# Output weights from three real products a direction, and the last quarter's Toeplitz blocks and early halves placed ahead of the late halves

## The chip, the cores and the metric

One core of one Trainium2 chip runs the kernel. The metric is the device time of one execution in microseconds (us); the kernel before took 1014.47 us, the median of three runs (1013.78 to 1017.83). The core has five instruction streams: PE (matmuls), DVE, ACT and POOL (element-wise work) and SP (which issues transfers only; ACT and POOL issue some as well). Each stream is executed in the order in which it was written, and streams wait for each other by semaphores.

## The reference

One layer: a bidirectional S5 mixer over 1024 tokens with a prefix of 256 context tokens, then a SwiGLU FFN and a final norm. The part that matters here is the S5 mixer, run once forward and once on the reversed sequence:

```python
lam_bar = jnp.exp(lam * jnp.exp(log_step)[:, None])
b_bar = ((lam_bar - 1.0) / lam)[..., None] * lax.complex(b_re, b_im)
bu = jnp.einsum('lgh,gnh->lgn', u, b_bar)
a = jnp.broadcast_to(lam_bar, bu.shape)
_, h = lax.associative_scan(_linear_combine, (a, bu), axis=0)   # h[l] = lam_bar h[l-1] + bu[l]
y = jnp.einsum('lgn,ghn->lgh', h, c_mat).real
...
g = jax.nn.gelu(y + d_skip * u)
return g * jax.nn.sigmoid(g @ w_glu + b_glu)
```

There are 64 groups of 16 channels with 64 complex states each. Everything is float32; the large matmuls run in fp32r with a high and a low part.

## The kernel before, in words

**Tokens and the scan.** The 1024 tokens stand as 128 columns of T = 8 tokens each. The recurrence runs over columns only (32 of context, 128 of tokens), both directions at once. After a loop of 16 blocks (`sums(hb)`, to about 123 us) has made each column's input, `scan()` runs on DVE alone: 95 steps of small TENSOR_TENSORs (L77 is the helper `tt`, which issues every TENSOR_TENSOR). A part of the columns is stepped through, the others are filled in from them on DVE and POOL.

**From states to outputs.** The groups come in eight parts k = 0..7 of 8, two parts to a quarter q = 0..3. A quarter needs three things. (1) Output weights `CL[q]`, one complex number for each direction, group, token of a column and channel: the complex output matrix C times powers of lam_bar. `cl_ops` makes them: a real or an imaginary part of one direction is the sum of two products of 128x1024, both made on POOL, one into its place and one into a scratch `ct`; with two directions that is eight products and four additions a quarter. (2) Lag matrices: `k_mats` (K) multiplies `CL[q]` by B-bar on PE (L809, L813, L817), ACT copies two results out (L821) and stores them to DRAM as `kd` (L822, issued by ACT); `toeplitz` (T, L830, issued by SP) reads them back as Toeplitz blocks into four slots `KQ`, two blocks for a k. (3) `x_mm` (L946) multiplies inputs by these blocks: the part of an output that comes from inside its own column. Then the states are multiplied by `CL[q]`: `states_mm` (L922) does one half of the columns, early or late; `states_all` (L935) does both. The backward direction needs a turned copy of the states (R early, Z late, z both; L902 on ACT, L904 on DVE).

**The additions of `cl_ops`** run on one of three engines, by a letter in the table `HOWS`: E on POOL itself; P on PE, as four identity matmuls into PSUM (L672) that ACT copies back (L673); Y by a DMA that POOL issues and that adds into its target (L675). Quarter 0 starts within the blocks of `sums`, with Y for its first two additions. In all POOL makes 9 additions, PE 5, the DMA 2.

**C's loads.** `cs_load(q)` (L, 512 KB, L651) reads C for a quarter into one of two buffers: real and imaginary part, then the same swapped. `cs_sign(q)` (G) flips the sign of three quarters of it on ACT (L655).

**The order** is written by hand: two strings, PROG1 (within the scan) and PROG2 (behind it), list operations by a letter and a number, and `run` issues them in that order, each to the streams of its engines. A: matmuls of the modulation on PE, whose weights SP loads. B: B-bar turned (PE L791, ACT L797). C: `cl_ops` by quarter and part, as C23. F: `fill` on POOL by quarter and half, as F31. P: x_mm and the early half of a k. Y: their copies out on ACT (L1001). N: a late half. D: its addition on DVE. H: GELU on ACT (L1010). Q: x_mm and both halves at once. I and J: transposes on PE (L1067) and their split into high and low part. O6: two cleared PSUM tiles for K6. M, m: the modulation's columns and rows. w, l: loads of w_glu. W: its casts (L1024, DVE). V: its low parts. x, g: gates and the GLU's first matmuls (L1107). In before k = 0..5 go by P and Y, then N and D; k = 6, 7 go whole by Q, behind N5.

## Time and profile before

| what | us |
| --- | --- |
| median of three runs | 1014.47 |
| profiled execution: its own time / its span | 1011.68 / 1009.9 |
| scan on DVE | 128.05 to 227.9 |
| first late half N0 on PE | 228.06 |
| x_mm of k = 6 on PE | 244.03 |
| first GLU matmul on PE | 257.05 |

Times of events are counted from the start of the span of the one profiled execution, whose own time is 1.8 us above its span and 2.8 below the median. A timeline row gives start, duration, engine, line, operation, output<-input, shapes and a count, and in brackets how long the engine was idle before it and what ended that. Buffer numbers are left out of names: `rxc` holds C, `rxa` the powers, `c` (in the streams `c_63` to `c_66`) the output weights of quarters 0 to 3, `rw` and a part of `c_66` scratch. A row of the busy time by stage gives the stretch, its length, then for PE, PE's weight loads, DVE, ACT and POOL the busy time and the number of instructions, and at the end the granted PE clock, the DMA engines' share and GB/s. In the page's first part shares are of the whole span.

### The profile page before, as it was taken

The page shows a single profiled execution, that of the slowest core. Times are in us where ns is not written, and L with a number is a line of the kernel's source. Part 1 is how long each engine was busy: PE and PEld are TensorE (multiplying, and loading weights), DVE is VectorE, ACT ScalarE, POOL GpSimd, SP SyncE. Part 2 cuts the span into 40 slices and gives each one's busy share as a digit, 9 for nine tenths or more (in the row PEclk, how much of TensorE's full clock was granted, in tenths as well). Part 3 has the DMA queues.
Part 4 walks back from the last instruction along what each step waited for, and adds up shares of the span by engine and source line. Part 5 has one row for each costly group of instructions (what it writes and reads, how often), then busy time and mean ns, then how long its engine had stood idle before and what let it go on. Part 6 is the DMA issues. An engine that isn't in the chain of part 4 may idle for free. (4 is left out here: it accounts for less than half of the span.)

```text
span 1009.9 us, 17677 instructions
## 1 busy us (share of the span) xinstructions
PE 956.2 (95%) x6604; PEld 749.3 (74%) x6604; DVE 779.8 (77%) x1595; ACT 431.1 (43%) x812; POOL 760.7 (75%) x589
## 2 busy tenths in 40 slices
...
DMA packets 48542, 98.90 MB, mean 98 GB/s; under 512 B 4284, under 2 KB 18876, under 8 KB 47176
## 3 DMA queue, kind: packets, MB, share of 16 engines
...
q14 instruction: 34, 0.28, 0.1%
...
## 5 line engine op out<-in xcount | busy, mean ns | idle before, releaser
L77 POOL TENSOR_TENSOR c<-rxc,c 128x512 fp32r<-128x512 f32 x127 | 165.8, 1318 | 52.3 <-ACT c L1248 51.5
L1307 PE MATMUL ut<-ra,c 128*128 128x512 f32 x400 | 155.7, 389 | 1.2 <-DVE ra L77 1.2
L1306 PE MATMUL ut<-ra,c 128*128 128x512 f32 x400 | 155.7, 389 | 0.2 <-ACT ra L1248 0.2
L1308 PE MATMUL ut<-ra,c 128*128 128x512 f32 x400 | 155.6, 389 | 0.0
L1248 ACT CAST c<-rxc 128x512 fp32r<-128x512 f32 x128 | 79.0, 622 | 147.6 <-PE xt L1601 53.0
L1601 PE MATMUL xt<-c,c 128*128 128x512 f32 x540 | 129.7, 389 | 0.0
L77 DVE TENSOR_TENSOR ru<-ru,xt 128x1024 f32<-128x1024 f32 x90 | 107.7, 1216 | 12.6 <-PE xt L1601 8.9
L1601 PEld LDWEIGHTS xt<-c,c 128*128 128x128 f32 x540 | 101.4, 188 | 21.0
L77 DVE TENSOR_TENSOR ru<-ut,ru 128x512 f32<-128x512 f32 x98 | 67.2, 687 | 44.2 <-PE ut L1308 38.7
L1307 PEld LDWEIGHTS ut<-ra,c 128*128 128x128 f32 x400 | 75.1, 188 | 17.1 <-POOL rxc L77 1.5
L1306 PEld LDWEIGHTS ut<-ra,c 128*128 128x128 f32 x400 | 75.1, 188 | 16.1 <-ACT ra L1248 0.6
L1308 PEld LDWEIGHTS ut<-ra,c 128*128 128x128 f32 x400 | 75.1, 188 | 15.6
L77 POOL TENSOR_TENSOR c<-rw,c 128x512 fp32r<-128x512 f32 (+1 forms) x28 | 37.9, 1353 | 37.6 <-ACT c L1248 37.6
L77 POOL TENSOR_TENSOR c<-ru,c 128x512 fp32r<-128x512 f32 (+1 forms) x39 | 58.2, 1492 | 10.1 <-ACT c L1248 5.7
L1306 PE MATMUL ut<-c,c 128*128 128x512 f32 x160 | 62.3, 390 | 0.8 <-DVE rxa L77 0.8
L1308 PE MATMUL ut<-c,c 128*128 128x512 f32 x160 | 62.3, 389 | 0.0
L1307 PE MATMUL ut<-c,c 128*128 128x512 f32 x160 | 62.2, 389 | 0.0
L77 POOL TENSOR_TENSOR rxc<-rxc 128x512 f32<-128x512 f32 x40 | 60.6, 1515 | 1.6
L1601 PE MATMUL ut<-c,c 128*128 128x512 f32 x216 | 51.9, 389 | 0.0
L584 PE MATMUL pv<-ru,c 128*64 128x160 f32 x512 | 44.0, 313 | 7.4 <-POOL ru L77 2.7
L77 DVE TENSOR_TENSOR ru<-ru,ut 128x512 f32<-128x512 f32 x76 | 47.3, 680 | 0.3
L77 POOL TENSOR_TENSOR c<-rxc,rxa 128x1024 f32<-128x1024 f32 x23 | 46.9, 2122 | 0.1
...
## 6 DMA issues: line engine op xcount, KB each, us to landing
...
```

The source lines that it names most:

```text
L77: eng.tensor_tensor(out=o, in0=x, in1=y, op=op)
L584: PE.matmul(pv[64 * (i % 2):64 * (i % 2) + 64, ri, c0:c0 + 160], w[:, i, 64 * ri:64 * ri + 64], U[:, 8 * b + 4 * j + i], start=True, stop= ...
L1248: S.copy(o[0], x)
L1306: PE.matmul(pu, wh, bh, start=start, stop=False)
L1307: PE.matmul(pu, wh, bl, start=False, stop=False)
L1308: PE.matmul(pu, wl, bh, start=False, stop=stop)
L1601: PE.matmul(pd, w[:, cs_], b, start=j in (1, 2, 4) and n == 0, stop=n == 2, skip_group_check=j not in (1, 2, 4))
```

## The change

**Three products in place of four.** With c2 = c0 − c1 and sums of the powers made beforehand, a direction's real and imaginary part are ct = c2 x p0 added to o0 = c1 x (p0 + p1) and to o1 = c0 x (p1 − p0), up to signs. So `cl_ops` works by direction, three products and two additions, and a quarter has six products in place of eight. The sums are made once, in `pw_sums` on DVE at block 12; c2 is made on POOL at the end of every `cs_sign`, behind ACT's sign flip, which shrinks to 128x256; C's loads shrink to 256 KB. By the new letters POOL makes 8 additions, PE 6, the DMA 2. ACT's copies of a P addition carry a scale of 1 or −1.

**Order.** T12 to T15 and R6 P6 Y12 Y13 R7 P7 Y14 Y15 stand at the end of PROG1, behind K7 K6 and F30 F31 and ahead of Z0 N0. Q6, Q7, z6, z7 go; N6 D6 N7 D7 Z6 Z7 come. P2 and P3 stand ahead of K4 and K5. W0 to W3 run on POOL. Some loads of w_glu stand earlier.

```diff
@@ -27,11 +27,10 @@
 NS = 64
 EPS = 1e-6
 MAGIC = 12582912.0
-HOWS = "PPPP PPEE PEEE EEEE"
+HOWS = "YPYP EPEP EPEP EEEE"
 ZEN = "VVSVSVSV"
-PROG1 = ("A22 B0 A26 C02 G1 A30 A34 C03 A40 K0 A44 A48 C10 K1 L2 A54 G2 C11 A60 F10 C12 F11 C13 T0 T1 T2 T3 A64 M0 M1 K2 R0 P0 Y0 Y1 K3 L3 R1 C20 P1 Y2 Y3 T4 T5 G3 T6 T7 C21 C22 C23 K4 R2 P2 Y4 Y5 K5 R3 P3 Y6 Y7 T8 T9 T10 T11 C30 C31 R4 P4 Y8 Y9 C32 C33 R5 P5 Y10 Y11 O6 K7 K6 M2 m0 F30 F31")
-PROG2 = ("T12 T13 T14 T15 Z0 N0 Z1 Z2 D0 Z3 N1 D1 Z4 H0 H1 N2 D2 H2 w0 w1 l1 N3 Z5 D3 H3 N4 D4 z6 z7 I0 J0 I1 J1 H4 N5 D5 I2 J2 H5 I3 J3 W0 W1 W2 W3 x0 x1 x2 x3"
-         " Q6 H6 I4 J4 Q7 I5 J5 V1 b0 w20 w21 l1 H7 g03 g13 I6 J6 g23 g05 g15 I7 J7 V2 g26 x10 x11 x12 x13")
+PROG1 = ("A22 B0 G1 C01 A26 A30 C03 A34 A38 K0 A42 C10 C11 K1 L2 T0 T1 T2 T3 A46 C12 C13 G2 A50 K2 F10 K3 L3 C20 A54 A58 F11 C22 R0 P0 Y0 Y1 T4 T5 R1 P1 Y2 Y3 T6 T7 A64 M0 M1 C21 G3 C23 R2 P2 Y4 Y5 R3 P3 Y6 Y7 K4 K5 T8 T9 T10 T11 C30 C31 C32 C33 R4 P4 Y8 Y9 R5 P5 Y10 Y11 O6 K7 K6 T12 T13 T14 T15 w0 l1 M2 m0 F30 F31 w1 R6 P6 Y12 Y13 R7 P7 Y14 Y15")
+PROG2 = ("Z0 N0 Z1 Z2 D0 Z3 N1 D1 Z4 H0 H1 N2 D2 Z5 H2 N3 D3 Z6 H3 N4 Z7 D4 H4 I0 J0 N5 D5 I1 J1 H5 W0 W1 N6 D6 I2 J2 H6 I3 J3 W2 W3 x0 x1 x2 x3 N7 D7 I4 J4 H7 V1 b0 w20 w21 l1 I5 J5 g03 g13 I6 J6 g23 g05 g15 I7 J7 V2 g26 x10 x11 x12 x13")
 LOG2E = 1.4426950408889634
 LN2H = 0.693359375
@@ -611,6 +610,17 @@
                 rot(*a_, V, (LTb, lbt[:, 256:512]))
 
         ptmp = [view(RXc, 2 + i, [256]) for i in range(2)]
+        ptmp2 = [view(RXc, i, [256]) for i in range(2)]
+        PS = [view(RXc, 3 + 4 * i, [T, 2, 16]) for i in range(2)]
+
+        def pw_sums():
+
+            for i in range(2):
+                gs = slice(16 * i, 16 * i + 16)
+                tt(PS[i], PWF[:, :, 0, :, gs], PWF[:, :, 1, :, gs], ADD)
+            b3, b2 = slice(24, 32), slice(0, 24)
+            tt(PWF[:, :, 1, :, b2], PWF[:, :, 1, :, b2], PWF[:, :, 0, :, b2], SUB)
+            tt(PWF[:, :, 1, :, b3], PWF[:, :, 0, :, b3], PWF[:, :, 1, :, b3], SUB)
 
...
@@ -645,39 +655,41 @@
             tt(STE[:, 31], STE[:, 31], ta, ADD)
             tt(STE[:, 31], STE[:, 31], tb, ADD)
 
-        Cs = [view(RXc, kb, [2, 2, 2, 8, HC]) for kb in (4, 0)]
+        Cs = [view(RXc, kb, [3, 2, 8, HC]) for kb in (4, 0)]
 
         def cs_load(q, eng=SY):
-            eng.dma_start(Cs[q % 2], a["cxy"][:, q])
+            eng.dma_start(Cs[q % 2][:, 0:2], a["cxy"][:, q])
 
         def cs_sign(q):
-            f = view(RXc, 4 - 4 * (q % 2), [1024])[:, 256:]
-            S.activation(f, f, AF.Copy, scale=-1.0)
+            c0, c1, c2 = (Cs[q % 2][:, i].rearrange("p d g h -> p (d g h)") for i in range(3))
+            S.activation(c1, c1, AF.Copy, scale=-1.0)
+            tt(c2, c0, c1, SUB, E)
 
         MB = view(RXa, 0, [D])
 
-        def cl_ops(q, part, ct, how):
-
-            ri, d = divmod(part, 2)
-
-            def prod(i, o, h=slice(0, 8), eng=E):
-                tt(o, bc(Cs[q % 2][:, i, ri, d, h], 2, T),
-                   bc(PWF[:, ::1 - 2 * d, i, d, 8 * q + h.start:8 * q + h.stop].rearrange("p t a -> p a t"), 3, HC), MUL, eng)
-
-            def add():
-                if how is PE:
+        def cl_ops(q, d):
+
+            ct, o0, o1 = cts[q][d], CL[q][:, 0, d], CL[q][:, 1, d]
+            gq = slice(8 * q, 8 * q + 8)
+            fac = [PWF[:, :, 0, d, gq], PS[q // 2][:, :, d, 8 * (q % 2):8 * (q % 2) + 8], PWF[:, :, 1, d, gq]]
+
+            def prod(i, o):
+                tt(o, bc(Cs[q % 2][:, (2, 1, 0)[i], d], 2, T), bc(fac[i][:, ::1 - 2 * d].rearrange("p t a -> p a t"), 3, HC), MUL, E)
+
+            def add(o, how, last):
+                if how == "P":
                     for h in range(2):
                         hs, pc = slice(4 * h, 4 * h + 4), pw([512])
                         for i, src in enumerate((o, ct)):
                             PE.matmul(pc, ident, src[:, hs].rearrange("p g t h -> p (g t h)"), start=i == 0, stop=i == 1)
-                        S.copy(o[:, hs].rearrange("p g t h -> p (g t h)"), pc)
-                elif how is SY:
+                        S.activation(o[:, hs].rearrange("p g t h -> p (g t h)"), pc, AF.Copy, scale=-1.0 if last else 1.0)
+                elif how == "Y":
                     E.dma_start(o, ct, accum_op=ADD)
                 else:
-                    tt(o, o, ct, ADD, E)
-
-            o = CL[q][:, ri, d]
-            return [lambda: prod(0, o), lambda: prod(1, ct), add]
+                    tt(o, o, ct, SUB if last else ADD, E)
+
+            h0, h1 = HOWS.split()[q][2 * d:2 * d + 2]
+            return [lambda: prod(0, ct), lambda: prod(1, o0), lambda: add(o0, h0, False), lambda: prod(2, o1), lambda: add(o1, h1, True)]
 
         PPAIR = (3, 5, 7, 8, 9, 11, 12, 13, 15)
...
-        cts = [[ct_[0], ct_[0], ct_[1], ct_[2]], [ct_[0], ct_[1], ct_[2], ct_[0]], [ct_[1], ct_[2], ct_[0], ct_[1]], [ct_[3], ct_[0]] * 2]
-        CL0 = cl_ops(0, 0, cts[0][0], SY) + cl_ops(0, 1, cts[0][1], SY)
+        cts = [[ct_[0], ct_[1]], [ct_[2], ct_[0]], [ct_[1], ct_[2]], [ct_[3], ct_[0]]]
+        CLP = {(0, d): cl_ops(0, d) for d in range(2)}
+        CL0 = [CLP[0, d].pop(i) for d, i in ((0, 0), (0, 0), (0, 0), (1, 1), (1, 0), (1, 0))]
         CLAT = {12: 1, 13: 1, 14: 2}
         for hb in range(16):
...
                 cs_sign(0)
+            if hb == 12:
+                pw_sums()
             for _ in range(CLAT.get(hb, 0)):
                 CL0.pop(0)()
...
                                       start=start and a_ + ri == 0, stop=stop and ri == 1 and a_ == 3)
 
-        def states_all(k, pts, hs):
-
...
                 elif op == "C":
                     q, part = divmod(i, 10)
-                    for f in cl_ops(q, part, cts[q][part], HOW[q][part]):
-                        f()
+                    if (q, part // 2) not in CLP:
+                        CLP[q, part // 2] = cl_ops(q, part // 2)
+                    fs = CLP[q, part // 2]
+                    for _ in range(len(fs) if part % 2 else 3):
+                        fs.pop(0)()
...
-                elif op == "z":
-                    turned(i, 2, HSq[i], ENG[ZEN[i]])
...
-                elif op == "Q":
-                    inner[i] = x_mm(i, pe8)
-                    states_all(i, inner[i], HSq[i])
...
-                    V.tensor_copy(view(W0[0], 4 * i, [1024]), wr0[i])
+                    E.tensor_copy(view(W0[0], 4 * i, [1024]), wr0[i])
...
         run(PROG1)
         psW.__exit__(None, None, None)
         psA.__exit__(None, None, None)
         psE = tc.tile_pool(name="psE", bufs=1, space=bass.MemoryType.PSUM, reuse_waits="tile")
         pE = psE.__enter__()
+        for _ in range(4):
+            pe8([512])
         run(PROG2)
```

Three places in the streams follow; a row has line, operation, output<-input, size, and the engines or queues that it waits for. The changed kernel's lines are shifted: its L76, L665, L685, L837, L845, L947 and L936 are L77, L655, L673, L822, L830, L946 and L922 of before.

POOL from the last DMA addition of quarter 0 into quarter 1 (L675, L687: that addition). Before:

```order
L77 TENSOR_TENSOR rw<-rxc,rxa 128x1024 [waits DMASW4_49]
L675 DMA c_63<-rw 128x1024 [waits DMASW5_49,Pool_49]
L77 TENSOR_TENSOR c_63<-rxc,rxa 128x1024 [waits DMAHW3_49,DMAHW4_49,DMASW1_49,PE_49]
L77 TENSOR_TENSOR c_66<-rxc,rxa 128x1024
L77 TENSOR_TENSOR c_63<-rxc,rxa 128x1024 [waits DMAHW5_49,DMAHW6_49,DMASW2_49,PE_49]
L77 TENSOR_TENSOR c_66<-rxc,rxa 128x1024 [waits DMAHW2_49,DMAHW1_49]
L77 TENSOR_TENSOR c_64<-rxc,rxa 128x1024 [waits DMAHW2_49,DMAHW0_49,DMAHW7_49,DMASW3_49,PE_49]
```

The same place in the changed kernel:

```order
L76 TENSOR_TENSOR c_66<-rxc,rxa 128x1024 [waits PE_49]
L687 DMA c_63<-c_66 128x1024 [waits DMASW5_49,Pool_49]
L76 TENSOR_TENSOR rxc<-rxc 128x256 [waits DMAHW2_49,Activation_49]
L76 TENSOR_TENSOR c_63<-rxc,rxa 128x1024 [waits DMAHW3_49,DMAHW4_49,DVE_49,PE_49]
L76 TENSOR_TENSOR c_63<-rxc,rxa 128x1024 [waits DMAHW5_49,DMAHW6_49,DMASW2_49,PE_49]
L76 TENSOR_TENSOR c_66<-rxc,rxa 128x1024 [waits DMAHW1_49,Pool_49]
L76 TENSOR_TENSOR c_64<-rxc 128x1024 [waits DMAHW0_49,DMAHW7_49,DMASW3_49,PE_49]
```

A 128x256 operation on `rxc`, which waits for ACT, now stands between the DMA addition and the next product: c2 of quarter 1. Quarter 1 itself (`c_64`) follows after two products in place of four.

POOL from the end of quarter 1 on (`ra<-ra,c_66` and `c_66<-ra,r_60` are a fill, 128x1024 are products and additions). Before:

```order
L77 TENSOR_TENSOR c_64<-rxc,rxa 128x1024 [waits DMASW7_49]
L77 TENSOR_TENSOR c_66<-rxc,rxa 128x1024 [waits PE_49,Pool_49]
L77 TENSOR_TENSOR c_66<-ra,r_60 128x256 [waits DVE_49]
...
L77 TENSOR_TENSOR c_64<-rxc,rxa 128x1024 [waits DMASW0_49]
L77 TENSOR_TENSOR c_66<-rxc,rxa 128x1024 [waits PE_49]
L77 TENSOR_TENSOR c_64<-c_64,c_66 128x1024 [waits Pool_49]
L77 TENSOR_TENSOR c_66<-ra,r_60 128x256 [waits DVE_49]
```

Changed:

```order
L76 TENSOR_TENSOR c_64<-c_64,rw 128x1024 [waits Pool_49]
L76 TENSOR_TENSOR c_64<-rxc,rxa 128x1024
L76 TENSOR_TENSOR rxc<-rxc 128x256 [waits DMAHW1_49,Activation_49]
L76 TENSOR_TENSOR c_66<-ra,r_60 128x256 [waits DVE_49]
...
L76 TENSOR_TENSOR c_66<-rxc,rxa 128x1024 [waits DMASW5_49,PE_49]
L76 TENSOR_TENSOR c_65<-rxc 128x1024 [waits DMAHW3_49,DMAHW2_49,PE_49]
L76 TENSOR_TENSOR c_65<-c_65,c_66 128x1024 [waits Pool_49]
```

c2 of quarter 2 stands ahead of the fill F10 and waits for a load and for ACT; before, quarter 1's products were interleaved with the two fills, and none of the rows waits for that load.

PE from K6 to N0 (L817 and L832: K6; `pe` in place of `pw` is the first late half, N0). Before:

```order
L809 MATMUL pw<-c_66,rxa 16x112 x30
L813 MATMUL pw<-r_60 16x16 x8
L817 MATMUL pw<-rxc,rxa 16x16 x32
L922 MATMUL pe<-c_63,ra 64x128 [waits DVE_49,Activation_49]
L922 MATMUL pe<-c_63,ra 64x128 [waits Activation_49]
L922 MATMUL pe<-c_63,ra 64x128 [waits DVE_49]
L922 MATMUL pe<-c_63,ra 64x128 x29
```

Changed:

```order
L828 MATMUL pw<-r_60 16x16 x8
L832 MATMUL pw<-rxc,rxa 16x16 x32
L947 MATMUL pw<-ra,ru 128x128 [waits DMAHW0_49,PE_49]
L947 MATMUL pw<-ra,ru 128x128 [waits Activation_49]
...
L947 MATMUL pw<-ra,ru 128x128 [waits DMAHW1_49]
...
L936 MATMUL pw<-c_66,ra 64x128 [waits Pool_49]
...
L936 MATMUL pw<-c_66,ra 64x128 [waits Activation_49]
...
L947 MATMUL pw<-ra,ru 128x128 [waits DMAHW2_49,PE_49]
...
L936 MATMUL pe<-c_63,ra 64x128 [waits DVE_49]
L936 MATMUL pe<-c_63,ra 64x128 [waits Activation_49]
```

x_mm of k = 6 and 7 (L947, each waiting for two loads of blocks) and their early halves (L936 into `pw`, waiting for POOL's fills and ACT's turned copies) now stand between K6 and N0; the rows left out hold the rest of them and the same six rows for k = 7.

35 lines of the change are left out of this document (9 added, 26 removed).

## The prediction

> **What bounds the kernel now.** I read the page's busy shares first, then the busy time by stage, then the timelines of POOL, ACT, SP and PE around the scan. Times are us from the span's start.
>
> ```profile
> PE 956.2 (95%) x6604; PEld 749.3 (74%) x6604; DVE 779.8 (77%) x1595; ACT 431.1 (43%) x812; POOL 760.7 (75%) x589
> ...
> 228.00:257.00 29.00, 28.94 (x695) 27.91 (x696) 18.11 (x26) 13.21 (x17) 11.75 (x14) 0.94 0.42 139
> 257.00:988.00 731.00, 727.25 (x3252) 600.40 (x3251) 539.22 (x711) 293.53 (x531) 539.98 (x392) 1.00 0.18 58
> ```
>
> From 228 on PE has no gap: 28.94 of 29.00 and 727.25 of 731.00. So whatever moves PE's first gate matmul (L1107, at 257.05) moves the end by the same amount; nothing later has slack to give it back. What moves that matmul is when PE starts the late halves (N0) and how much it does from there on.
>
> ```profile
> 227.62 0.29 DVE L77 TENSOR_TENSOR ra<-ltc,ra 128x128 f32<-128x128 f32 x1
> ...
> 228.06 11.88 PE L922 MATMUL pe<-c,ra 64*64 64x128 f32 x320 [1.26 <-ACT r L821]
> ...
> 240.90 2.27 PE L922 MATMUL pe<-c,ra 64*64 64x128 f32 x64
> ...
> 244.03 1.95 PE L946 MATMUL pe<-ra,ru 128*128 128x128 f32 x16
> 245.91 4.25 PE L935 MATMUL pe<-c,ra 64*64 64x128 f32 x128
> ...
> 257.05 0.47 PE L1107 MATMUL pe<-c,c 128*128 128x512 f32 x1
> ```
>
> The scan's last step ends at 227.9 and N0 starts 0.15 behind it: DVE's scan sets N0, and PE, ACT and POOL prepare inside the scan's 100 us. Of these POOL is full in three stretches (25.60 of 25.80, 23.05 of 23.30, 25.32 of 25.70):
>
> ```profile
> 131.20:157.00 25.80, 25.36 (x235) 7.69 (x229) 25.73 (x145) 6.81 (x13) 25.60 (x19) 1.00 0.98 327
> 157.00:172.80 15.80, 12.77 (x184) 4.07 (x183) 15.80 (x91) 3.37 (x7) 14.17 (x12) 0.92 0.76 257
> 172.80:196.10 23.30, 19.04 (x481) 13.75 (x478) 23.30 (x134) 7.65 (x18) 23.05 (x12) 0.98 0.34 99
> 196.10:221.80 25.70, 22.96 (x608) 20.28 (x608) 24.26 (x107) 8.54 (x19) 25.32 (x12) 1.00 0.36 103
> 221.80:234.40 12.60, 9.82 (x426) 9.33 (x430) 9.20 (x30) 5.19 (x9) 12.21 (x20) 0.86 0.28 81
> ```
>
> **What the change takes off PE behind N0.** k = 6, 7 were done whole behind the scan (two x_mm L946, two states_all L935, rows above); now only their late halves are. A half is the step 240.90 to 243.10, 2.2. So 2 x 1.9 of x_mm and 2 x (4.2 − 2.2) leave: 7.7. N0 to gates was 257.05 − 228.06 = 29.0 and becomes 21.3. That is the most the change can gain, and it gains only if N0 starts before 228.1 + 7.7 = 235.8.
>
> **What it puts ahead of N0.** On PE, ahead of N0 in program order: x_mm 6, early half 6, x_mm 7, early half 7. x_mm 6 waits for Toeplitz blocks T12, T13, which wait for kd stores of K7 and K6, which wait for the last output weight C33; the halves wait for F30, F31 on POOL. In before that latency lay under N0 to N5:
>
> ```profile
> 228.01 0.33 ACTq L822 DMA_DIRECT2D kd<-r  x1
> ...
> 229.78 5.18 SPq L830 DMA_DIRECT2D ra<-kd  x4
> ```
>
> The store ends at 228.3, the four loads are issued from 229.8, and x_mm 6 ran at 244.03. The loads' packets fell between 231.5 and 239.7 (mine, from 229.78 and the issue's 5.18: second block after about 7, fourth after about 11). So the whole forecast hangs on when POOL delivers C33 and PE reaches K7 and K6.
>
> **POOL, saved.** Of 32 products 24 are left, of 9 adds 8; the wait for a DMA-add and the wait on a scan step go too.
>
> ```profile
> 128.26 2.01 POOL L77 TENSOR_TENSOR rw<-rxc,rxa 128x1024 f32<-128x1024 f32 x1 [2.76 <-DMA c<-rw]
> ...
> 160.74 1.41 POOL L77 TENSOR_TENSOR c<-ra,r 128x256 f32<-128x256 f32 x2 [1.36 <-DVE ra L77]
> ...
> 172.84 7.96 POOL L77 TENSOR_TENSOR c<-rxc,rxa 128x1024 f32<-128x1024 f32 x4
> ...
> 202.59 2.03 POOL L77 TENSOR_TENSOR c<-rxc,rxa 128x1024 f32<-128x1024 f32 x1
> ...
> 209.02 2.02 POOL L77 TENSOR_TENSOR c<-rxc,rxa 128x1024 f32<-128x1024 f32 x1
> ...
> 219.51 2.36 POOL L77 TENSOR_TENSOR c<-c,rw 128x1024 f32<-128x1024 f32 x1
> ```
>
> 8 x 1.98 (the steps of 7.96 by four) = 15.8, one add 2.35, waits 2.76 and 1.36: 22.3.
>
> **POOL, added.** c2 = c0 − c1 once a quarter, 128x256, by the row below 0.73 each: 2.9. It sits in cs_sign, behind ACT's sign flip, and everything on POOL queues behind it. That gives three new waits.
>
> ```profile
> L77 POOL TENSOR_TENSOR ra<-ra,rxc 128x256 f32<-128x256 f32 x7 | 5.1, 727 | 0.3
> ...
> 133.88 1.07 ACT L797 COPY c<-pw 128x512 f32<-128x512 f32 x2 [0.69 <-PE pw L791]
> ...
> 162.14 0.44 ACTq L651 DMA_DIRECT2D rxc<-in_cxy  x1
> 168.76 0.84 ACT L655 ACTIVATE rxc<-rxc 128x768 f32<-128x768 f32 x1 [7.01 <-DMA rxc<-in_cxy]
> ...
> 134.73 3.70 PE L672 MATMUL pw<-c,r 128*128 128x512 f32 x8
> ...
> 138.47 0.59 ACT L673 COPY c<-pw 128x512 f32<-128x512 f32 x1 [1.13 <-PE pw L672]
> ```
>
> Quarter 1: POOL is free at 129.1 (128.26 − 2.76 + one c2 and its product), but the flip stands on ACT behind bb_put's copies, which end at 134.95 when PE's B0 feeds them. Flip (128x256, half of the 0.84) to 135.4: POOL waits 6.3. Then c2, and by 2.0 a product, 6.4 for two products with a POOL add (the step 202.59 to 209.02), 4.4 for one with an add: C01 138.1, C03 140.1, C10 146.5, C11 148.5, C12 154.9, C13 156.9.
>
> Quarter 2: its weights are loaded behind K1. PE's queue from 138.2: C01's add 3.45 (the row's 3.70 less the pipeline's tail), A26 and A30 2.0, C03's add 3.45, A34 and A38 2.5, K0 1.7, A42 1.0, C11's add 3.45 to 155.75; ACT's copies and zeros to 157; K1 to 158.8; two copies with kd stores to 160.4; then the load. The row's 512 KB took 162.14 to 168.7; now 256 KB, for which no row of that place stands: 5.5 taken, bounds 3 (half) and 6.6 (the same). Flip done 166.4, against POOL's 156.9: it waits 9.6 (7 to 11).
>
> The Trainium skill's "SBUF — State Buffer", The DMA setup-cost knee, has about 2 us plus bytes at 436 GB/s for a load; for 256 KB that is an estimate of 2.6, the flip would be done at 163.5 and the sum would be 2.9 lower. The row's 6.6 for 512 KB, where that rule gives 3.2, and the DMA engines' 0.76 share in that stretch speak against it.
>
> Before, POOL had C12, F11 and C13 to do in those 7.01 us in which ACT alone waited; now c2 stands ahead of F10. On: F10 (5.8) 173.0, C20 179.4, F11 185.2, C22 191.6, C21 193.6.
>
> Quarter 3: C21's add now goes over PE and ACT; its copies end 4.3 behind 193.7 (138.47 + 0.59 − 134.73), 198.0, and the flip stands behind them: 198.4. POOL waits 4.9; c2 199.2, C23 201.2, C30 207.6, C31 212.1, C32 218.5, C33 222.9, then M2, F30 229.4, F31 235.3.
>
> ```profile
> 221.81 0.20 POOL L888 COPY r<-r 128x8 f32<-128x8 f32 x1
> ...
> 222.40 1.41 POOL L77 TENSOR_TENSOR rw<-ra,r 128x256 f32<-128x256 f32 x2
> ...
> 228.10 1.84 POOL L77 TENSOR_TENSOR rw<-ra,r 128x256 f32<-128x256 f32 x2
> ...
> 232.76 1.64 POOL L77 TENSOR_TENSOR ra<-ra,rw 128x256 f32<-128x256 f32 x2
> ```
>
> Before, C33 ended at 221.8 and F31 at 234.3 (F30, the step 222.40 to 228.10, is where a fill's 5.7 comes from; 5.8 with its slack). So 22.3 saved, 2.9 added and 20.8 waited: POOL ends about 1 us later than before.
>
> **PE's ladder ahead of N0.** Row for K and for the copies out:
>
> ```profile
> 196.14 0.27 PE L809 MATMUL kt<-c,rxa 64*16 64x112 f32 x1 [1.29 <-POOL c L77]
> ...
> 197.67 0.17 PE L817 MATMUL pm<-rxc,rxa 64*16 64x16 f32 x1
> ...
> 197.78 2.34 PE L946 MATMUL pw<-ra,ru 128*128 128x128 f32 x16
> ...
> 220.46 1.07 ACT L1001 COPY ru<-pw 128x512 f32<-128x512 f32 x2 [4.09 <-PE pw L946]
> ```
>
> K4 ran at 196.14 as soon as POOL had q = 2. Now C23 (201.2) goes to PE for its add (204.75), and P2, P3 stand ahead of K4: x_mm 2.1 and half 2.2 each, to 209.0 and, with the turned copy between, 214.0. K4 215.6, K5 218.5 (it waits for K4's ACT copies), stores done 220.0. SP's T8 to T11 wait for them: second block 7 later, 227, fourth 230.8. P4 done 228, its copies, R5, P5 234 (before: 221). Then K7, K6 237.6 and stores 239.1 (before: 228.3, though C33 came at about the same time). T13 246, x_mm 6 247, half 249.2, x_mm 7 251.9 (T15 at 249.8), half 254.1, Y14's copy, **N0 at 254.5**, 26.4 later.
>
> Sum: 26.4 − 7.7 = 18.7 on the profiled execution's 1011.68 (span 1009.9 and 1.8 around it): 1030.4. The runs' median, 1014.47, is 2.8 above that execution: 1033.2 there. I take 1032.
>
> **Costed at nothing.** pw_sums on DVE at hb 12, four TENSOR_TENSORs of 128 to 384 elements, about 1.7 by the 0.43 of 256:
>
> ```profile
> 115.45 0.43 DVE L77 TENSOR_TENSOR ltb<-ra,lta 128x256 f32<-128x256 f32 x1 [5.30 <-ACT ra L593]
> ...
> 246.69 1.57 DVE L1024 CAST c<-rxa 128x1024 fp32r<-128x1024 f32 x1
> ```
>
> The 5.30 hides it; without that cover the scan and N0 shift by at most 1.7. The sign in the ACT copies replaces a copy of the same size. W0 to W3 leave DVE (the row of L1024, 1.6 each) for POOL, idle behind F31; the nearest two-operand row of 1024, 2.36, bounds it: 9.4 from N5 on, with the gates waiting at most 1.6. PE's clock was 0.86 in 221.8:234.4 behind its short waits; the longer ones ahead of N0 can repeat that, up to 1.7. Both are in the upper end only.
>
> **Rivals.** (1) *POOL's relief passes through.* With the flips early (ACT idles for 4 to 7 us at a time there, "[7.01 <-DMA" above) and no wait at c2, C23 ends at 201.2 − 20.8 = 180.4, K4 to P7 close before 228 and N0 follows the scan as now: 1011.7 − 7.7 = 1004, about 1007 on the median. For it: POOL's three full stretches, which the change shortens by 8 products. The Trainium skill's "Perfetto Trace Analysis", Identifying the Most-Contended Engine, would have the engine of highest occupancy improved first; in these stretches POOL is among the fullest, so by that rule the change gains. Against: the flip's place on ACT behind bb_put and behind C21's copies, and the load behind K1. It decides at C23 by 183: more than 18 of the 20.8 would have to be missing. 0.09.
>
> (2) *POOL waits, but PE's ladder overlaps.* If K7 and K6 run as soon as C33 is there (223) as in before, T13 lands by 236 and x_mm 6 follows F31 at 235.3: 8.4 of P6 and P7, N0 243.7, +7.9: 1020, 1022 on the median. Against it: P5's blocks in the same four slots. 0.18.
>
> (3) *No difference.* Load at 3 us, ladder overlapped, only P7's half behind F31: N0 237.5, +1.7: 1013.4 to 1016. 0.10.
>
> (4) *Worse.* The casts, the clock and 1 us more on each of the four loads of the ladder (two of cxy, two of kd) all charged: 1032 + 1.6 + 1.7 + 4 = 1039. 0.05.
>
> **Numbers.** The ladder as summed has 0.58 and its own range 1024 to 1039. To hold 8 in 10 the range takes in case (2): 1016 to 1040. A difference of 0.5%, 5 us, is what can be told here from none. Faster is case (1), 0.09; same is (3), 0.10; slower the rest, 0.81.
>
> **What would show it.** The scan still ends at 227.9. POOL waits before each 128x256 `rxc<-rxc`, for ACT, of about 6, 10 and 5, at 129, 157 and 194. K4's first L809 form near 214 in place of 196, K7's near 234. Two waits of PE for `ra<-kd`, before 227 and before 245. N0 near 254, the first gate matmul near 276, then the same 731 to the end. If POOL reaches F30 by 210, or N0 starts below 240, the ladder is wrong.

## The result: 2.9% slower

The changed kernel takes **1043.03 us**, the median of six runs (1039.01 to 1045.54), against 1013.68 for the kernel before in the same series: a ratio of 1.0289, 95% interval 1.027 to 1.0309. The sign and the mechanism are those of the forecast; the size is not. 1032 was predicted with 1040 as the upper end, and the time lies 3 above that end. The profiled execution, the fastest of the six, took 1039.01 with a span of 1037.2, against 1030.4 in the prediction's sum.

The busy time by stage of the changed kernel (columns as in the prediction: PE, its weight loads, DVE, ACT, POOL, then the granted PE clock, the DMA share and GB/s):

```profile
223.20:236.00 12.80, 9.81 (x136) 8.57 (x134) 5.53 (x19) 1.59 (x3) 11.83 (x20) 0.65 0.34 83
236.00:264.00 28.00, 18.09 (x478) 16.45 (x470) 0.00 (x0) 5.88 (x14) 0.00 (x0) 0.79 0.52 165
264.00:285.00 21.00, 20.97 (x539) 19.81 (x540) 14.09 (x24) 13.75 (x18) 7.88 (x8) 1.00 0.03 10
285.00:1016.00 731.00, 726.80 (x3247) 599.81 (x3247) 540.03 (x713) 294.02 (x532) 541.43 (x393) 1.00 0.18 58
```

The last row is the one from 257.05 on in the kernel before: 726.80 of 731.00 against 727.25. Nothing changed there. From 264 to the gates PE is full. The scan on DVE ends at 227.6, as before; what was lost lies between there and 264, where N0 starts, and from 236 on POOL and DVE do nothing and PE works 18.09 of 28.00. POOL's timeline has the three new waits in their places, and C33's last operation:

```profile
135.42 0.71 POOL L76 TENSOR_TENSOR rxc<-rxc 128x256 f32<-128x256 f32 x1 [4.47 <-ACT rxc L665]
167.09 0.73 POOL L76 TENSOR_TENSOR rxc<-rxc 128x256 f32<-128x256 f32 x1 [10.24 <-ACT rxc L665]
198.84 0.72 POOL L76 TENSOR_TENSOR rxc<-rxc 128x256 f32<-128x256 f32 x1 [4.77 <-ACT rxc L665]
220.86 2.35 POOL L76 TENSOR_TENSOR c<-c,rw 128x1024 f32<-128x1024 f32 x1
```

C33 ends at 223.2, where 222.9 was forecast. PE's timeline behind it shows the ladder:

```profile
228.16 1.16 PE L947 MATMUL pw<-ra,ru 128*128 128x128 f32 x8 [1.92 <-DMA ra<-kd]
230.07 1.78 PE L947 MATMUL pw<-ra,ru 128*128 128x128 f32 x8 [0.75 <-DMA ra<-kd]
...
236.73 2.28 PE L947 MATMUL pw<-ra,ru 128*128 128x128 f32 x16
...
251.86 3.79 PE L947 MATMUL pw<-ra,ru 128*128 128x128 f32 x16 [7.89 <-DMA ra<-kd]
255.59 3.07 PE L936 MATMUL pw<-c,ra 64*64 64x128 f32 x64
...
264.03 10.21 PE L936 MATMUL pe<-c,ra 64*64 64x128 f32 x318 [0.45 <-ACT ru L999]
...
283.82 0.47 PE L1101 MATMUL pe<-c,c 128*128 128x512 f32 x1
```

N0 starts at 264.03 (before: 228.06), the first gate matmul, from here on "the gates", at 283.82 (before: 257.05). ACT's timeline gives the loads and stores between (ACTq rows are its DMA issues):

```profile
162.50 0.44 ACTq L661 DMA_DIRECT2D rxc<-in_cxy  x1
166.59 0.42 ACT L665 ACTIVATE rxc<-rxc 128x256 f32<-128x256 f32 x1 [0.71 <-DMA rxc<-in_cxy]
...
217.54 0.90 ACTq L837 DMA_DIRECT2D kd<-r  x1
...
221.19 1.02 ACTq L837 DMA_DIRECT2D kd<-rw  x1
...
245.18 0.51 ACTq L837 DMA_DIRECT2D kd<-r  x1
```

K4's and K5's stores are done at 222.2, K7's and K6's at 245.7; x_mm of k = 6 starts 6.2 behind the latter.

### The profile page after: what moved, and what is told of

It is laid out like the page before. It is cut to its first block, busy times and chain, and to the rows that moved or that the text cites. A ratio compares the mean times of both kernels' runs of the same rounds, so it can differ in the third digit from the quotient of the medians.

```text
span 1037.2 us, 17705 instructions
## 1 busy us (share of the span) xinstructions
PE 963.2 (93%) x6612; PEld 756.1 (73%) x6612; DVE 779.1 (75%) x1599; ACT 434.4 (42%) x818; POOL 748.9 (72%) x588
## 5 line engine op out<-in xcount | busy, mean ns | idle before, releaser
L76 POOL TENSOR_TENSOR c<-rxc,c 128x512 fp32r<-128x512 f32 x127 | 166.2, 1322 | 53.8 <-ACT c L1243 52.9
L76 DVE TENSOR_TENSOR ru<-ru,xt 128x1024 f32<-128x1024 f32 x90 | 107.7, 1216 | 12.6 <-PE xt L1596 8.9
L76 DVE TENSOR_TENSOR ru<-ut,ru 128x512 f32<-128x512 f32 x98 | 67.2, 687 | 43.0 <-PE ut L1303 37.5
L76 POOL TENSOR_TENSOR rxc<-rxc 128x512 f32<-128x512 f32 (+1 forms) x44 | 64.4, 1464 | 22.7 <-ACT rxc L665 21.1
L76 POOL TENSOR_TENSOR c<-ru,c 128x512 fp32r<-128x512 f32 (+1 forms) x39 | 58.2, 1492 | 10.1 <-ACT c L1243 5.7
L76 POOL TENSOR_TENSOR c<-rw,c 128x512 fp32r<-128x512 f32 (+1 forms) x28 | 37.8, 1351 | 37.6 <-ACT c L1243 37.6
L76 DVE TENSOR_TENSOR ru<-ru,ut 128x512 f32<-128x512 f32 x76 | 47.3, 680 | 0.3
L1596 PEld LDWEIGHTS ut<-c,c 128*128 128x128 f32 x216 | 40.6, 188 | 8.4
```

Of the source, the lines that this page charges most:

```text
L76: eng.tensor_tensor(out=o, in0=x, in1=y, op=op)
L1596: PE.matmul(pd, w[:, cs_], b, start=j in (1, 2, 4) and n == 0, stop=n == 2, skip_group_check=j not in (1, 2, 4))
```

## The experiments

Theory at the start: N0 is held by the ladder C33, P4, P5, K7 and K6, store and reload, x_mm and halves of k = 6, 7; what holds the ladder are POOL's waits and K4, K5 behind P3. Rivals: a low PE clock in the ladder, and the moved blocks and halves by themselves. Ratios are to the kernel before on the same chip, with 95% intervals; places are from each run's profiled execution. "The move" is the second half of the change: the blocks and the early halves of k = 6, 7 ahead of N0. "Late" in a name says that k = 6, 7 are done whole behind N5, as in the kernel before.

### The two halves of the change apart

**b1_moved** is the kernel before, with four products, and only the second half of the change. W0 to W3 stay on DVE.

```diff
-K7 K6 M2 m0 F30 F31
+K7 K6 T12 T13 T14 T15 w0 l1 M2 m0 F30 F31 w1 R6 P6 Y12 Y13 R7 P7 Y14 Y15
...
-T12 T13 T14 T15 Z0 N0
+Z0 N0
...
-x3 Q6 H6 I4 J4 Q7 I5 J5
+x3 N7 D7 I4 J4 H7
```

> The kernel before, four products and its own order up to F31, with only the second half of the change: T12 to T15, R6 P6 Y12 Y13 R7 P7 Y14 Y15 ahead of N0 and the changed kernel's second string; W on DVE. POOL has no c2 and no new wait. Theory (the halves ahead of N0 expose the blocks' way through DRAM even with POOL as before): kd out at 228, blocks at 235, N0 at 245 to 249, less 7.7 behind it: 10 to 13 us slower than before, time 1023 to 1028. Rival (only POOL's waits make the ladder late): N0 at 236 or earlier, time 1014 or less.

Measured: 1025.89, ratio 1.0125 (1.0099 to 1.015), as the theory expected. PE's timeline:

```profile
234.94 2.05 PE L945 MATMUL pw<-ra,ru 128*128 128x128 f32 x8 [7.54 <-DMA ra<-kd]
...
246.02 10.11 PE L921 MATMUL pe<-c,ra 64*64 64x128 f32 x320
...
265.71 0.47 PE L1106 MATMUL pe<-c,c 128*128 128x512 f32 x1
...
275.99 0.50 PE L1107 MATMUL pe<-c,c 128*128 128x512 f32 x1 [3.38 <-DVE c L76]
```

N0 comes 18.0 later, 9.3 of it comes back up to the gates, so the move costs 8.7 there even without any of POOL's new waits. The other 5.3 of this execution's span (+14.0) arise behind the gates. DVE, which has the casts W here, delivers a low part late there, and PE waits 3.38 for it in one row; that all of the 5.3 belong to the casts was not shown. The changed kernel has these casts on POOL, and its gates wait at most 0.5 for DVE.

**e4_q67late** is the reverse: the changed kernel with three products, and k = 6, 7 whole behind N5 as in before.

```diff
-K7 K6 T12 T13 T14 T15 w0 l1 M2 m0 F30 F31 w1 R6 P6 Y12 Y13 R7 P7 Y14 Y15
+K7 K6 M2 m0 F30 F31
...
-Z0 N0
+T12 T13 T14 T15 Z0 N0
...
+                elif op == "Q":
+                    inner[i] = x_mm(i, pe8)
+                    states_all(i, inner[i], HSq[i])
```

> The changed kernel (three products, c2, its order up to F31) with k = 6 and 7 done whole behind N5 as in the kernel before, T12 to T15 at the head of the second string: N0 no longer stands behind the last blocks. Theory: N0 follows K6 near 245, then 29.0 us to the first gate matmul in place of 20 to 21: gate matmul near 274 in place of 284, time 1032 to 1035. So of the 29 us lost about 10 belong to putting P6 and P7 ahead of N0, the rest to what comes before. Rival (putting them ahead costs nothing, the ladder before it is all): time 1041 to 1052, since 8 us of PE work come back behind N0.

Measured: 1034.74, 1.0197 (1.0171 to 1.0224), the time as expected, N0 at 249.9 and not near 245. PE's timeline:

```profile
249.93 12.59 PE L937 MATMUL pe<-c,ra 64*64 64x128 f32 x318 [0.59 <-ACT r L836]
...
279.75 0.47 PE L1126 MATMUL pe<-c,c 128*128 128x512 f32 x1
```

The three products in this order cost 1.97% with nothing moved, and the move 0.92% on top. Each half is slower alone. If the 5.3 us (0.5%) behind the gates are put down to the casts and taken out of b1_moved's 1.25, the two alone make 2.7 of the 2.89 together.

### POOL's waits

**e1_signs** puts flip and c2 together at other places; **e5_split** takes them apart (G is the flip on ACT, S is c2 on POOL) and puts each c2 behind other work of POOL, each flip early.

```diff
-B0 G1 C01 A26 A30 C03 A34
+B0 C01 A26 A30 C03 G1 A34
...
-C13 G2 A50 K2 F10 K3 L3 C20 A54 A58 F11 C22
+C13 F10 F11 G2 A50 K2 K3 L3 C20 A54 A58 C22
...
-C21 G3 C23
+G3 C21 C23
```

> The changed kernel with c2 and the sign flip put where POOL has other work: G1 behind C03, G2 behind F10 and F11, G3 ahead of C21. Nothing else moves. Theory (POOL's three waits of 4.5, 10.2 and 4.8 us pass down the whole ladder): the waits before rxc<-rxc 128x256 shrink to under 2 us each, C33 ends near 204 in place of 223, N0 starts 17 to 20 us earlier (244 to 247 in place of 264), time 1023 to 1026 against the 1043 of the changed kernel. Rival (PE's ladder of K4, P4, P5, K7, K6, P6, P7 sets N0 by itself, POOL's waits lie beside it): N0 moves by less than 6 us, time 1037 or more.

e1_signs: 1041.6, 1.0282 (1.0256 to 1.0307). It says nothing on what the waits are worth, since they only moved; behind C03 the flip stands behind ACT's copies of C03's addition. POOL's timeline:

```profile
145.64 0.73 POOL L76 TENSOR_TENSOR rxc<-rxc 128x256 f32<-128x256 f32 x1 [10.46 <-ACT rxc L665]
```

e5_split, against the changed kernel:

```diff
-B0 G1 C01 A26 A30 C03 A34
+B0 G1 C01 A26 A30 C03 S1 A34
...
-C13 G2 A50 K2 F10 K3 L3 C20 A54 A58 F11 C22
+C13 G2 F10 F11 S2 A50 K2 K3 L3 C20 A54 A58 C22
...
-T4 T5 R1 P1 Y2 Y3 T6 T7 A64 M0 M1 C21 G3 C23
+T4 T5 G3 R1 P1 Y2 Y3 T6 T7 A64 M0 M1 S3 C21 C23
```

> The changed kernel with the flip on ACT and c2 on POOL taken apart (c2 gets its own letter S): the flips stay early on ACT (G1 behind B0, G2 behind C13, G3 between Y1 and R1), c2 stands later on POOL (S1 behind C03, S2 behind F10 and F11, S3 ahead of C21). The ladder of PE is left as it is. The run before this one only moved the waits (10.5, 0 and 4.6 us in place of 4.5, 10.2 and 4.8), so this is its question asked again. Theory (POOL's waits pass down the ladder): waits before rxc<-rxc under 2 us each, C33 at 203 to 206 in place of 223, N0 at 242 to 247 in place of 264, time 1020 to 1026. Rival (PE's ladder from P2 to P7 sets N0 by itself): C33 early as well, but N0 at 258 or later, time 1037 or more.

e5_split: 1029.54, 1.0165 (1.0144 to 1.0185), 13.5 less than the changed kernel. POOL's timeline:

```profile
135.53 0.73 POOL L76 TENSOR_TENSOR rxc<-rxc 128x256 f32<-128x256 f32 x1 [0.46 <-ACT rxc L666]
...
181.58 0.74 POOL L76 TENSOR_TENSOR rxc<-rxc 128x256 f32<-128x256 f32 x1 [1.05 <-ACT rxc L666]
...
185.87 4.00 POOL L76 TENSOR_TENSOR c<-rxc,rxa 128x1024 f32<-128x1024 f32 x2 [3.55 <-PE pm L530]
```

The waits for a flip are at most 1.1 now, and C33 ends at 211.5, 11.7 earlier (203 to 206 was expected). N0 comes only 9.7 earlier, at 254.3 where 242 to 247 was expected: PE's ladder does not pass on all that POOL gives, and C21 waits for A64, whose weights lie where C21 writes.

### The order of K4, K5 and P2, P3

**e2_kfirst** puts K4 and K5 ahead of P2 and P3 in the changed kernel; **e6_split_kfirst** does so in e5_split.

```diff
-R2 P2 Y4 Y5 R3 P3 Y6 Y7 K4 K5 T8 T9 T10 T11
+K4 K5 R2 P2 Y4 Y5 T8 T9 R3 P3 Y6 Y7 T10 T11
```

> The changed kernel with only K4 and K5 put ahead of P2 and P3 (T8 T9 behind P2, T10 T11 behind P3); POOL's waits stay. Theory (P2 and P3 ahead of K4 cost PE's ladder their 9 us): K4 near 207 in place of 216, P4 near 219 in place of 228, and since K7 and K6 then wait for C33 at 223, N0 9 to 11 us earlier, time 1032 to 1035. Rival (the ladder is set by POOL's C33 and F31 alone): N0 within 2 us of 264, time 1041 to 1045.

> The same as the run with flip and c2 apart, and K4 and K5 ahead of P2 and P3. In the changed kernel K first gained nothing because C33's last product writes where P3's turned copy lies and then waited 7 us for P3; with POOL's waits gone P3 is done (about 198) before C33 gets there (about 204). Theory: K4 at 186 to 190, P4 at 199 to 205, kd of K6 out by 214, N0 at 230 to 236, time 1009 to 1016, that is no slower than before. Rival (the two orders interlock whatever POOL does): a wait <-PE before C33's product, N0 at 242 or later, time 1020 or more.

e2_kfirst: 1039.77, 1.0251 (1.0223 to 1.028), N0 at 264.4: missed. P3 is now late, and its turned states lie where C33's product is written. POOL's timeline:

```profile
229.48 2.11 POOL L76 TENSOR_TENSOR c<-rxc,rxa 128x1024 f32<-128x1024 f32 x1 [7.04 <-PE pw L936]
```

What K gains, C33 loses. e6_split_kfirst: 1024.15, 1.011 (1.0088 to 1.0131), N0 at 249.2, with a wait of 5.20 at the same place, C33. So the change's P2, P3 ahead of K4, K5 is one side of a trade, not a slip: either order delays something that the ladder needs.

**e8_split_kfirst_late** was meant as e6_split_kfirst with k = 6, 7 late. As run it has K4, K5 behind P3, against its name and its expectation; its pair is e5_split.

> The changed kernel with the flips apart from the subtractions and with K4, K5 ahead of P2, P3, and k = 6, 7 whole behind N5 as in before. With the blocks and early halves still ahead of N0 this order took 1024.15, N0 at 249.2, and its x_mm of k = 6 had waited 7.67 since 229.6. If the two halves of the change are two terms that overlap only in that wait, N0 now comes right behind K6, at 229.5 to 231, gates at 259 to 261, 1013 to 1019, and about 8 less than with them. Rival (the order around C33, P3 and K6 itself holds N0, the moved halves fill its gaps): N0 stays behind 236, 1020 or more.

Measured: 1019.41, 1.0064 (1.0045 to 1.0082), N0 from 231.6 on, the gates at 262.4: a little behind what was expected of the other order. Against e5_split the move costs 1.0%.

These two have the same order up to K6, yet K6's last store is done at 237.5 in e5_split and at 233.2 here. When K5's stores were done they were 1.5 apart (212.7 and 211.2); then P5's half took 3.70 and 2.25, its x_mm 2.73 and 2.04. The busy time by stage, first of e5_split:

```profile
210.00:223.00 13.00, 8.41 (x104) 7.28 (x87) 12.14 (x51) 1.41 (x4) 12.61 (x20) 0.50 0.38 102
223.00:236.00 13.00, 11.23 (x370) 9.77 (x369) 5.79 (x23) 3.87 (x9) 0.47 (x1) 0.74 0.07 22
```

and of e8_split_kfirst_late:

```profile
210.00:223.00 13.00, 9.25 (x104) 8.24 (x108) 12.14 (x51) 2.56 (x5) 12.38 (x20) 0.59 0.55 131
223.00:236.00 13.00, 10.16 (x402) 9.29 (x400) 5.84 (x23) 5.49 (x11) 0.00 (x0) 0.93 0.16 53
```

With gaps in PE's work the granted clock was 0.50 and 0.74 in the one execution and 0.59 and 0.93 in the other, and a ladder of dependent steps carries the longer rows to its end. The changed kernel and e4_q67late also have the same order up to K6, and their last stores are done at 245.7 and 250.3. So single profiles of such kernels are good to some 4 us here, and sums of places to no better.

### The clock

**e3_warm** and **e3b_warm** fill PE's gaps at P4 and ahead of x_mm 6 with identity matmuls that nothing reads: 20 and 44, then 9 and 26.

```diff
-C33 R4 P4
+C33 X9 R4 P4
...
-K7 K6 T12
+K7 K6 X26 T12
...
+                elif op == "X":
+                    xp = pw([P])
+                    for _ in range(i):
+                        PE.matmul(xp, ident, ident, start=True, stop=True)
```

> The changed kernel with matmuls of the identity by itself added on PE in two idle stretches ahead of N0: 20 ahead of P4, 44 behind K6; they write a tile that nobody reads. Theory (the 9.5 us by which N0 came later than I had summed are PE's clock, 0.65 and 0.79 granted in 223:236 and 236:264, because PE idles there): x_mm of k = 6 takes 2.0 in place of 3.8 and the halves 2.2 in place of 3.1, the granted clock of the last stretch is over 0.9, N0 is 3 to 6 us earlier, time 1037 to 1040. Rival (the clock is a sign of waiting, not a cause): N0 and the time within 1 us, or later by what the added matmuls take.

> The changed kernel with 9 matmuls of the identity by itself ahead of P4 and 26 behind K6 (in the run with 20 and 44 they took 10 us behind K6 and pushed x_mm of k = 6 back by 8, but it then took 1.95 in place of 3.79 and the half 2.27 in place of 3.07). These should end before the blocks land. Theory (PE's lowered clock is the part of the ladder that I had left out): x_mm of k = 6 2.0, halves 2.3, N0 2 to 5 us earlier than 264, time 1038 to 1041 against 1043. Rival (the clock costs nothing that the waits don't hide): 1042 to 1045.

e3_warm: 1045.51, 1.0314 (1.0295 to 1.0332); the fillers outlast the gaps, x_mm 6 starts at 260.1. e3b_warm: 1040.13, 1.0277 (1.0242 to 1.0312), not to be told from the changed kernel's 1.0289. Its stage row and PE's timeline:

```profile
236.00:264.00 28.00, 23.44 (x594) 21.62 (x590) 0.00 (x0) 7.16 (x16) 0.00 (x0) 1.00 0.53 161
```

```profile
252.21 1.13 PE L947 MATMUL pw<-ra,ru 128*128 128x128 f32 x8 [0.25 <-DMA ra<-kd]
254.03 1.16 PE L947 MATMUL pw<-ra,ru 128*128 128x128 f32 x8 [0.70 <-DMA ra<-kd]
...
263.24 10.21 PE L936 MATMUL pe<-c,ra 64*64 64x128 f32 x318 [0.94 <-ACT ru L1003]
```

The clock is 1.00 in place of 0.79 and x_mm 6 takes 1.13 and 1.16, but its second block is there only at 254.0, and N0 comes 0.8 earlier. Where x_mm waits for blocks, the slow clock costs little. Over the whole ladder it costs more: this execution was 2.6 behind the changed kernel's when K5's stores were done (224.8 against 222.2, ahead of the fillers), and from there to N0 it took 38.4 in place of 41.8. By one execution of each, then, the clock is worth some 3.4 of the ladder, and not the whole 9.5.

### An order without the waits

**v1**, **v2** and **v3_late** were tries at an order without any of these. v1 and v3_late have K4 right behind C23, A64 ahead of R1, K7 ahead of R5, and F30, F31 around C33, with their scratch moved within `rw`. v1 and v2 (e6_split_kfirst's order) put only the early halves of k = 6, 7 ahead of N0, with x_mm behind it; their x_mm of k = 6 reads inputs over which Y14 and Y15 have already been written, so its values differ, while work and order are what they would be, and only their time is read. The scratch is moved in v2 too, though its expectation says that only x_mm moves. v3_late has k = 6, 7 whole behind N5.

```diff
-R1 P1 Y2 Y3 T6 T7 A64 M0 M1 C21 G3 C23 R2 P2 Y4 Y5 R3 P3 Y6 Y7 K4 K5 T8
+A64 M0 M1 R1 P1 Y2 Y3 T6 T7 S3 C21 C23 K4 R2 P2 Y4 Y5 K5 R3 P3 Y6 Y7 T8
...
-C32 C33 R4 P4 Y8 Y9 R5 P5 Y10 Y11 O6 K7 K6
+C32 F30 C33 F31 R4 P4 Y8 Y9 K7 R5 P5 Y10 Y11 K6
...
-                    fill(*divmod(i, 10), *((RW, 0) if i >= 30 else (RC[3], 12)))
+                    fill(*divmod(i, 10), *((RW, 4) if i >= 30 else (RC[3], 12)))
```

> A version of the change in which nothing ahead of N0 waits for the blocks: three products, flip and c2 apart, A64 ahead of P1, K4 ahead of P2 and K5 ahead of P3, F30 between C32 and C33 and F31 behind it (with scratch of their own), K7 between P4 and P5. For k = 6 and 7 only the early half stands ahead of N0; x_mm goes with the late half into N6 and N7, 15 us behind N0. Theory (what the change could gain is only PE work that fits ahead of the scan's end: 2 x 2.2 of early halves; the blocks' way must lie under other work): C33 at about 214, F31 at 220, N0 at 228 to 231, first gate matmul 24.6 behind it, time 1009 to 1013. Rival (PE's ladder of k = 2..5 ends too late even so): N0 at 234 or later, time 1015 or more.

> The earlier run with flip and c2 apart and K4, K5 ahead of P2, P3 (1024 us), with one thing changed: x_mm of k = 6 and 7 leaves the place ahead of N0 and goes with the late half into N6 and N7. Nothing of POOL's work or of the ladder up to K6 moves. Theory (of that run's 11 us over the kernel before, most is PE standing for the last blocks): N0 at 233 to 236 in place of 249, x_mm's 3.8 come back behind N0, time 1012 to 1017. Rival (PE would be late anyway): 1020 or more.

> The same order as in the first of these runs up to K6, but k = 6 and 7 whole behind N5 as in the kernel before: three products without the moved halves. Theory (in the kernel before the scan alone sets N0, so that what POOL saves is worth nothing by itself): N0 within 2 us of 228, the same 29.0 to the first gate matmul, time within 3 us of the kernel before. Rival (POOL bounds the kernel before, and fewer products are worth time by themselves): 1009 or less.

v1: 1020.13, 1.0078 (1.0057 to 1.01). v2: 1025.46, 1.0119 (1.0102 to 1.0135). v3_late: 1018.12, 1.0047 (1.0029 to 1.0065). All three missed, by one collision: the fills' new scratch lies in the place from which K7's and K5's copies are stored. POOL's timeline of v2 and ACT's of v3_late:

```profile
227.64 1.58 POOL L76 TENSOR_TENSOR rw<-ra,r 128x256 f32<-128x256 f32 x2 [10.62 <-DMA kd<-rw]
```

```profile
221.99 0.36 ACT L838 COPY rw<-kt 128x240 f32<-128x240 f32 x1 [6.25 <-POOL ra L76]
```

**v4_late** and **v4_move** put F30, F31 and their scratch back behind C33. v4_late, whose edit against v3_late is shown, has k = 6, 7 whole behind N5; v4_move has the second half of the change again (T12 to Y15 behind K6 as in the changed kernel).

```diff
-C32 F30 C33 F31 R4
+C32 C33 R4
...
-K6 M2 m0
+K6 M2 m0 F30 F31
...
-                    fill(*divmod(i, 10), *((RW, 4) if i >= 30 else (RC[3], 12)))
+                    fill(*divmod(i, 10), *((RW, 0) if i >= 30 else (RC[3], 12)))
```

> As v3_late, but F30 and F31 behind C33 with their scratch where it was, so that it no longer lies in K7's staging. C33 then ends at about 211, K7's ACT copies no longer wait 6.25 for POOL, K6 is done before 226 and the scan alone sets N0: 228 to 229, 1010 to 1016, ratio 0.997 to 1.003. Theory: three products without POOL's waits are worth nothing by themselves, since the scan ends at 227.9 as before. Rival (POOL's relief passes through): below 1009. Rival (another stall follows): N0 behind 231, 1016 to 1019.

> The order of v4_late with the second half of the change back: T12 to T15 and early halves of k = 6, 7 ahead of N0. K6's store at 222 to 225, second block 7 later, x_mm of k = 6 at 230 to 232, fourth block 4 later, N0 at 238 to 244; gates 20 behind, 258 to 264; 1012 to 1021. It beats before only with N0 ahead of 236.7 (228 + the 8.7 between 29.0 and 20.3), which this order does not reach by the sum. Rival (with C33 ten us earlier the ladder fits under the scan): N0 below 234, 1009 or less.

v4_late: 1013.76, **1.0005** (0.9991 to 1.002). v4_move: 1019.95, **1.0075** (1.0051 to 1.0099). Both times are as expected. PE's timeline of v4_late:

```profile
229.22 9.40 PE L939 MATMUL pe<-c,ra 64*64 64x128 f32 x278 [0.47 <-ACT r L838]
...
259.07 0.47 PE L1128 MATMUL pe<-c,c 128*128 128x512 f32 x1
```

Three products, with waits for a flip of at most 1.8, equal four products. C33 ends at 212.4 in place of 221.8, and the time is the same. By the Trainium skill's "Perfetto Trace Analysis", Identifying the Most-Contended Engine, the engine of highest occupancy is optimized first; in the first three of the prediction's five rows that is DVE (25.73, 15.80 and 23.30 us against POOL's 25.60, 14.17 and 23.05), and v4_late agrees in so far as relieving POOL by 9.4 us ahead of its last handover moved the time by 0.05%, with an interval that holds zero. A shorter scan was not tried.

POOL was nearly full, but N0 can't start ahead of the scan's end on DVE. In the trace N0 is freed by ACT, which copies K6's results out behind PE's ladder. ACT's timeline before, then ACT's and DVE's of v4_late (the scan's last step):

```profile
227.62 0.36 ACT L821 COPY r<-pw 128x240 f32<-128x240 f32 x1 [0.40 <-ACT r L821]
```

```profile
228.81 0.36 ACT L838 COPY r<-kt 128x240 f32<-128x240 f32 x1 [0.78 <-PE pm L834]
```

```profile
227.33 0.29 DVE L76 TENSOR_TENSOR ra<-ltc,ra 128x128 f32<-128x128 f32 x1
```

Before, that copy ends at 227.98, 0.07 behind the scan. In v4_late it ends at 229.17, 1.55 behind the scan, although C33 came 9.4 earlier: PE had P5 to do until 227.1 and K6 behind it. So two things end together at 228, the scan and the ladder to K6. POOL's relief moved neither, and the scan alone leaves nothing to gain ahead of 228.

PE's timeline of v4_move:

```profile
232.80 3.85 PE L949 MATMUL pw<-ra,ru 128*128 128x128 f32 x16 [7.60 <-DMA ra<-kd]
...
243.92 10.71 PE L938 MATMUL pe<-c,ra 64*64 64x128 f32 x320
...
264.22 0.47 PE L1103 MATMUL pe<-c,c 128*128 128x512 f32 x1
```

The move still costs 0.7% (against v4_late) although C33 comes 12 us earlier than in the changed kernel. **v5_move** puts P5 under the store and reload.

```diff
-R4 P4 Y8 Y9 K7 R5 P5 Y10 Y11 K6 T12 T13 T14 T15
+R4 P4 Y8 Y9 R5 K7 K6 T12 T13 P5 Y10 Y11 T14 T15
```

> As v4_move, but K7, K6 and the loads T12, T13 ahead of P5 (R5 ahead of K7), so that the store and reload of quarter 3's lag matrices begin some 8 earlier and P5 lies under them. In v4_move K6's last store was issued at 226.7 and x_mm of k = 6 started 6.1 behind. Now: K6's last store at 218 to 220, second block 224 to 226, x_mm 6 and its half to 230, T14 and T15 behind P5's x_mm (223) at 230, N0 at 233 to 236, gates 20.3 behind at 253 to 256 against 257.05 before: 1008 to 1013. Break-even is N0 at 236.7. Theory (the move pays once the reload has work over it): at or slightly below before, ratio 0.995 to 1.000. Rival (ACT's or PE's queue holds P5 or the stores elsewhere): N0 stays behind 240 and the ratio above 1.003.

Measured: 1016.37, 1.0026 (1.0012 to 1.0041), better than v4_move and still not below before; the expected 1008 to 1013 was missed. ACT's and PE's timeline:

```profile
223.24 0.92 ACTq L839 DMA_DIRECT2D kd<-r  x1
```

```profile
230.14 1.13 PE L949 MATMUL pw<-ra,ru 128*128 128x128 f32 x8 [2.33 <-DMA ra<-kd]
232.08 1.56 PE L949 MATMUL pw<-ra,ru 128*128 128x128 f32 x8 [0.81 <-DMA ra<-kd]
...
241.22 10.09 PE L938 MATMUL pe<-c,ra 64*64 64x128 f32 x320
...
260.90 0.47 PE L1103 MATMUL pe<-c,c 128*128 128x512 f32 x1
```

K6's last store is done at 224.2, 4 to 6 later than expected; from there everything follows at the usual distance. Over the kernels with the move (a store counts from the end of its issue):

| kernel | last store done | x_mm 6 starts | N0 | store to N0 | N0 to gates |
| --- | --- | --- | --- | --- | --- |
| changed | 245.7 | 251.9 | 264.0 | 18.3 | 19.8 |
| b1_moved | 228.9 | 234.9 | 246.0 | 17.1 | 19.7 |
| e5_split | 237.5 | 243.0 | 254.3 | 16.8 | 19.8 |
| e6_split_kfirst | 231.1 | 237.3 | 249.2 | 18.0 | 20.0 |
| v4_move | 226.7 | 232.8 | 243.9 | 17.2 | 20.3 |
| v5_move | 224.2 | 230.1 | 241.2 | 17.1 | 19.7 |

N0 follows the last store by 17 to 18: 5.4 to 6.2 of store and reload, and 11 to 12 of x_mm, half, x_mm, half and the copy out. The gates were at 257.05 before, so the move pays only with N0 ahead of 237.3 (257.05 − 19.7) and so with the last store ahead of about 220. That counts from one execution of the kernel before, which is 2.8 below its median; v4_late, which is no slower than before, has its gates at 259.07, and by it the limit is some 2 later. The best order here stored at 224.2, behind a C33 that ended at 213.8. That an order with a store by 220 exists was not shown. No version faster than the kernel before was found.

## Why the prediction was right and wrong

**Right: what bounds.** The scan still ended where it did (227.6), the 731 us from the gates on are the same, and the loss is all ahead of N0. "DVE's scan sets N0" is half of it: the row shown there has N0 freed by ACT's copy of K6, which ended 0.07 behind the scan. The sum did not suffer from that.

**Right: POOL.** The waits were forecast as 6.3, 9.6 and 4.9 and came as 4.47, 10.24 and 4.77; C33 and F31 were 0.3 and 0.1 later than summed. One agreement is luck: quarter 2's load was issued 2.1 later than summed (162.50 against 160.4) and took 4.1 to the flip, where 5.5 had been taken. The Trainium skill's "SBUF — State Buffer", The DMA setup-cost knee, gave an estimate of 2.6 for it; the row of 6.6 for twice the bytes was the safer side, and 4.1 lies between.

**Right: costed at nothing.** pw_sums stayed under DVE's wait, of which 3.11 were left. The casts W on POOL took 1.04 each and no gate waited for them; in b1_moved, which has them on DVE, 5.3 are lost behind the gates.

**Wrong: the step "PE's ladder ahead of N0".** It put N0 at 254.5; it came at 264.03, 9.5 later. Each row of the ladder was a little short, and the errors added up, since every step waits for the one before:

| end of | forecast | measured | added here |
| --- | --- | --- | --- |
| stores of K4, K5 | 220.0 | 222.2 | 2.2 |
| P4 | 228 | 231.85 | 1.6 |
| P5 | 234 | 239.0 | 1.2 |
| stores of K7, K6 | 239.1 | 245.7 | 1.6 |
| x_mm 6 | 247 | 255.65 | 2.0 |
| its half | 249.2 | 258.65 | 0.8 |
| N0 | 254.5 | 264.03 | 0.1 |

Four terms of the sum were mis-sized.

*K on PE.* K7 and K6 were summed at 3.6 behind P5 (234 to 237.6) and took 5.0 (239.0 to 244.0); K4 and K5 were summed at 4.5 behind P3 (214 to 218.5) and took 6.0 (213.9 to 219.9). The kernel before has that size in its own rows: behind C33 its K7 and K6 took 4.9 (221.9 to 226.8). PE's timeline before, the start of K7 behind C33 and the end of K6, then the end of K6 in the changed kernel:

```profile
221.92 0.27 PE L809 MATMUL kt<-c,rxa 64*16 64x112 f32 x1 [0.94 <-POOL c L77]
...
226.05 0.75 PE L817 MATMUL pw<-rxc,rxa 64*16 64x16 f32 x62
```

```profile
243.22 0.75 PE L832 MATMUL pw<-rxc,rxa 64*16 64x16 f32 x62
```

Within K6 PE stands 1.40 before and 1.34 here, for which the profile shows no wait; why stays open.

*The stores.* K5's second store took ACT 1.02 to issue, where 0.33 was summed by the row of K6. The kernel before has other rows too: K2's and K3's second stores took 1.00 and 1.12 there.

*The second block.* It came not 7 but about 8 behind the last store: 230.07 − 222.21 = 7.9 for P4, and 232.08 − 224.16 = 7.9 for x_mm 6 in v5_move, where x_mm waits for it in a row of its own.

*PE's clock.* It fell to 0.65 and 0.79 in the ladder, priced at 1.7 in the upper end only. P5's half took 3.70 where 2.25 is the row before, the half of k = 6 took 3.07 where 2.2 was summed. Within x_mm 6 it counts for less: 3.79 here and 1.13 and 1.16 with a wait between in e3b_warm, but from the last store to x_mm's end that is 10.0 against 9.3, most likely because both wait for the second block.

Taken from these rows, K makes about 2.9 of the 9.5, the stores 1.0, the second blocks 2.1 and the clock 3.4. The split is an estimate from one execution.

**Somewhat better than forecast:** N0 to gates came as 19.8, not 21.3: the matmuls of N0 to N4 took 10.21 in place of 11.88, at a granted clock of 1.00 in place of 0.94. The profiled execution was so 8.6 above its sum. The median lies 4.0 above it where 2.8 was added, and 1032 was 1.2 below the sum itself.

**The rivals.** (1), POOL's relief passing through, asked for C23 by 183, and no run reached that. v4_move comes nearest, with waits for a flip of at most 1.0, C23 at 193.7 and N0 at 243.9, and is 0.75% slower than before; the same relief without the move (v4_late) gains nothing. (2) and (3) asked for the ladder to overlap; v5_move, in which POOL's waits are away as well, is the nearest case, at 1016.37, close to (3)'s 1013.4 to 1016. The changed kernel does not have that order. (4) charged clock and transfers and reached 1039: the right direction, and still 4 short on the median.

**What is shown and what is not.** Shown: both halves cost alone (b1_moved, e4_q67late); taking the flips' waits away, with the fills and c2 at other places, is worth 1.2% here (e5_split); three products cost and gain nothing where POOL hardly waits for a flip (v4_late); the move costs 0.7 to 1.0% in three orders with the casts on POOL, and in the fourth, v5_move, the kernel is 0.26% slower than before. Between e4_q67late and v4_late lie 1.9%, which the waits and the order of K4 to K7 share; how, was not taken apart, since these orders hold each other by shared places.
